# Lower weight parts in 256-column pieces only in the head stages, conditioning columns moved into the chunk stage, scan and exponentials queued behind the head

## The chip, the cores and the metric

One core of a Trainium2 chip runs the whole program. The metric is the device time of one execution in microseconds (us); the time before is the median of three runs. Engines are named as in the profile: PE (matmuls), PEld (weight loads), DVE (vector), ACT (scalar), POOL (GpSimd), SP (issues most DMAs).

## What is computed

A trunk of two layers on x (1 x 512 x 1024), all in float32. In each layer a vector c gives three conditioning vectors of 1024 (shift, scale, gate); two token mixers (HGRN2, 4 heads of 128; RWKV-7, 8 heads of 64) work on parts of one projection, and sigmoid gates merge them:

```python
for l in range(DEPTH):
    cond = jax.nn.silu(c) @ w_ada[l] + b_ada[l]
    shift, scale, gate_raw = jnp.split(cond, 3, axis=-1)
    h = x * (1.0 + scale[:, None]) + shift[:, None]
    proj = h @ w_in[l]
    p_hg, p_rw, p_gate = jnp.split(proj, [HG_COLS, HG_COLS + RW_COLS], axis=-1)
    ...
    o_hg = hgrn2_chunked(q, k_hg, i_val, log_f)
    y_rw = rwkv7_scan(r, decay, k, v, kk, a)
    ...
    merged = jax.nn.sigmoid(g_hg) * y_hg + jax.nn.sigmoid(g_rw) * y_rw
    out = merged @ w_out[l]
    x = layer_norm(DN_ALPHA * x + (1.0 + gate_raw[:, None]) * out, ln_g[l], ln_b[l])
```

## The kernel before

Activations lie transposed, 128 features on the partitions and 512 tokens in the free dimension. Every large product is split in two parts: a weight tile `raw` (128x512, four 128x128 blocks) is loaded by SP, ACT rounds it into a higher part `wh` (L122 or L244), POOL subtracts to get the lower part `wl` (L248, recorded at the helper line L127), and PE adds three matmuls per block: `wh` by the higher and lower part of the activation (L267, L268), and `wl` by the higher part (L272). Eight matmuls with `wh` come first, then four with `wl`. There are three buffers each of `raw`, `wh` and `wl`. POOL makes the lower part in pieces of 256 columns:

```python
for i in range(0, n, 256):
    x = slice(i, i + 256)
    tt(G, lo[:, x], raw[:, x], hi[:, x].bitcast(F32), ALU.subtract)
```

A layer has these stages, each a chain of small dependent work ("main") with projection matmuls woven in as filling by hand-written counts (`weave`):

- **Heads**, p = 0 to 3: `hg_head` (HGRN2 head p) and then `rw_prep` (what RWKV-7 needs for two of its heads). A head ends with a masked copy of scores (COPY_PREDICATED, L781), a copy of the last block (L806), transposes and their copy out of PSUM (L813), the state product on PE (L818), its copy (L820), two recurrent steps on DVE (L136, tile `u`) and the output product (L828, L831). In `rw_prep` DVE makes a running sum of the decays (L430, TENSOR_TENSOR_SCAN), ACT two exponentials of it (L433 into `ep`, L434 in place; both recorded at L124), and DVE the products that PE multiplies at L497. There is one buffer `ep` for all pairs of heads.
- **Inverse** of small triangular blocks (`rw_invert`) and **chunks**, c = 0 to 7 (`rw_chunk`): the recurrence of RWKV-7 over chunks of 64 tokens. In a chunk DVE scales `W` (L618), PE multiplies it (L623), the result is copied into `X`, one half by DVE and the other by ACT (L625), PE multiplies `X` (L631, L643), and DVE adds into the state `mbd` (L636, L638). The chunks are given a higher priority by 1000.
- **Branches**: for j = 0 to 7 the two branch products, the gated sum on DVE (L147, L1149), and the first half of the output product; POOL has four lower parts per j. Then the layer boundary with its norm, or the end.

The conditioning vectors are made column by column on DVE: a group is one (vector, block of 128 rows), two loads of 128x512 of `w_ada` (256 KB each, L327) and two halves, each a multiply-and-sum over 512 columns with silu(c) (`ada_col`, L308, CUSTOM_DVE in the profile), and an addition. `ada_next` computes the groups that are loaded and loads the next ones. Where a group stands in the program is set by tables of numbers: in layer 0 thirteen groups over the heads (`WAZ`) and eleven over the branches (`WAB`), in layer 1 eight over the heads (`WAO`), none in the chunks. silu(c) lies in the buffers of `mbd` and `W`, which the chunks need.

The order on each engine is made by a list scheduler from the order of the program and its own estimates. `tc.issue_after(i)` keeps what stands under it behind instruction i; without it, an instruction whose inputs are there may be put far ahead of its place in the code.

Of the kernel before, what the change touches and what calls it, by code (L numbers as in the profile page):

```python
# [18 lines left out]

WAZ = (1, 0, 2, 2, 2, 2, 2, 2)  # L20
WAO = (1, 1, 0, 1, 1, 2, 0, 2)
WAB = (2, 1, 2, 1, 2, 1, 2, 1, 1)
NWARM = 5
# [60 lines left out]
def body(ctx, tc, d):  # L84
# [41 lines left out]
    def tt(e, o, a, b, op):  # L126
        e.tensor_tensor(o, a, b, op=op)  # L127

    def mul(e, o, a, b):
        tt(e, o, a, b, ALU.mult)  # L130

# [108 lines left out]


    def split(raw, hi, lo):

        act(hi, raw, AF.Copy)  # L244
        n = raw.shape[-1]
        for i in range(0, n, 256):
            x = slice(i, i + 256)
            tt(G, lo[:, x], raw[:, x], hi[:, x].bitcast(F32), ALU.subtract)  # L248
# [69 lines left out]

    def ada_next(*groups):

        for g, w in pend:
            ada_col(*g, w)
        pend[:] = []
        for l, n, k in groups:
            w = [st("z", [128, 512]) for _ in range(2)]
            for h in range(2):
                nc.sync.dma_start(w[h], d["w_ada"][l, n, k, :, h * 512:(h + 1) * 512])  # L327
            pend.append(((l, n, k), w))

    def gate_rows(l):  # L330
# [85 lines left out]

    def rw_prep(l, p, r, k, v):
        sg, th = rw["gt"][p][:, 0], rw["gt"][p][:, 1]
# [10 lines left out]
        cum = pu()  # L429
        V.tensor_tensor_scan(cum, mask64, sg, 0.0, ALU.mult, ALU.add)  # L430
        EP = ep
        EI = cum
        act(EP[:, :, 1:65], cum.rearrange("p (c j) -> p c j", j=64), AF.Exp, scale=-KAPPA)  # L433
        act(EI, cum, AF.Exp, scale=KAPPA)  # L434
        G.tensor_copy(gam[:, p], EP[:, :, 64])
# [134 lines left out]

    def rw_chunk(l, c):

# [43 lines left out]
        for g in range(2):  # L616
            z, o = zrs[g], halves[g]
            mul(V, j3(W[z, o]), j3(py[z, o]), bc(d2[z, c4, 2 * g:2 * g + 2].rearrange("p a b -> p (a b)"), 64))  # L618
        yield
# [4 lines left out]
        for g in range(2):  # L624
            PK[1 - g](X[zrs[g], halves[g]], psa[zrs[g], halves[g]])  # L625
        yield
        if c < 7:
            pm = ps("rw")
            for p in range(4):
                for h in range(2):  # L630
                    mm(pm[64 * h:64 * h + 64, hcol(p, h)], bkt[:, hcol(p, h)], X[:, hcol(p, h)], start=p == 0, stop=p == 3)  # L631
            for h in range(2):
                hs = slice(64 * h, 64 * h + 64)
                new = pm[hs].rearrange("p (a b) -> p a b", b=128)[:, :, hs]
                if c == 0:
                    V.tensor_copy(mbd[hs, :, hs], new)  # L636
                else:
                    tt(V, mbd[hs, :, hs], new, gm[hs], ALU.add)  # L638
                if c < 6:
                    mul(G, gm[hs], mbd[hs, :, hs], bc(gam[hs, :, c + 1], 64))  # L640
        for n, (p, h) in enumerate(heads):
            y = yrs[p // 2]
            mm(py[y, hcol(p, h)], Gt[:, h, p, y], X[:, hcol(p, h)], start=False, stop=n > 5, skip_group_check=True)  # L643
# [81 lines left out]

    def hg_head(l, hd, src, outs):

# [38 lines left out]
        for n, H in enumerate(HG_LEVELS):  # L766
# [11 lines left out]
            for c in range(2):  # L778
                mm(pS[:, c * 128:(c + 1) * 128], kp[:, c * 128:(c + 1) * 128], ql[:, c * 128:(c + 1) * 128],
                   start=c == 0, stop=c == 1)  # L780
            V.copy_predicated(late(acc), hmask[:, n].rearrange("p (c b j) -> p c b j", c=4, j=H),  # L781
                              pS[:, 0:256].rearrange("p (c b j) -> p c b j", c=4, j=H))
# [29 lines left out]
        kt = u()  # L812
        A.copy(kt[:, 0:384], pT[:, 0:384])  # L813
        yield
# [173 lines left out]
    for l in range(L):  # L988
# [53 lines left out]
        if l == 0:  # L1042
            hgp = [hg_f(l, 0, fout[1]), hg_q(fout[2])]
            wad = rw_wa0(l, fout[0])
            hgp.append(hg_i(fout[3]))
            act(gh0, fout[6], AF.Tanh, scale=0.5)
            rkv = [rw_in(l, 4, fout[4]), rw_in(l, 0, fout[5])]
        else:
            hgp = [hg_f(l, 0, fout[2]), hg_q(fout[3])]
        for p in range(NP):  # L1050
            early = []
# [4 lines left out]
            else:  # L1056
                fill = itertools.chain(krv(p, rkv), rw_wa(l, wad), fqi(1, early, 1))
            weave(hg_head(l, p, hgp, oT), fill, (WHL if l else WHZ, WHG if l else WHS, WHG, WHG)[p])
            run(fill)
            ada_next(*itertools.islice(ada, (WAZ, WAO)[l][2 * p]))  # L1060
            if p == 0:
# [4 lines left out]
            else:  # L1066
                fill = itertools.chain.from_iterable(
                    [gate(j) for j in range(5)] + [zrw(p) for p in range(NP)] + [zhg(p) for p in range(NP)] +
                    [gate(j) for j in range(5, KT)])
            weave(rw_prep(l, p, rkv[1], rkv[0], rkv[2]), fill, WPR)  # L1070
            ada_next(*itertools.islice(ada, (WAZ, WAO)[l][2 * p + 1]))
            if p < 3:
                run(fill)
            rkv = []
        ada_next()
        G.memset(mbd, 0.0)
        inv = rw_invert()
# [293 lines left out]
```

## Time and profile before

| | |
|---|---|
| median of 3 runs | 1013.33 us (1008.05 to 1017.07) |
| the profiled execution | 1013.57 us, span 1011.8 us |
| PE busy | 939.3 us (93%) |
| DVE busy | 711.7 us (70%) |
| POOL busy | 632.4 us (63%) |
| ACT busy | 452.2 us (45%) |
| DMA, mean | 112 GB/s |
| granted PE clock, mean | 0.991 |

The span is the time from the first instruction to the last; 1.8 us lie around it. Busy shares are means over stages that differ: the idle time of PE, 72.5 us in all, is what a change of order can win, and the views by stage say where it lies. A clock of 1.00 is the level of 2.4 GHz, and 0.5 that of 1.2 GHz.

### The profile page before, as it was taken

What the parts mean: (1) busy time and instruction counts of PE and PEld (TensorE: products, weight loads), DVE (VectorE), ACT (ScalarE), POOL (GpSimd) and SP (SyncE); (2) the same over time, 40 slices, a digit from 0 to 9 for tenths busy, and PEclk for the clock granted to TensorE, in tenths of its full rate; (3) what the DMA queues carried; (4) which work ended last, traced back from release to release, by engine and by line L of the source; (5) the groups of instructions that cost most, each with busy time, mean ns of one, the idle gap of its engine ahead of it and who ended that gap; (6) DMA issues with size and microseconds to landing.
All of it is one profiled execution on the core that took longest, in us unless ns stands there. A gap on an engine that the chain in (4) does not pass through costs nothing.

```text
span 1011.8 us, 17028 instructions
## 1 busy us (share of the span) xinstructions
PE 939.3 (93%) x6132; PEld 751.6 (74%) x6132; DVE 711.7 (70%) x1265; ACT 452.2 (45%) x920; POOL 632.4 (63%) x738
## 2 busy tenths in 40 slices
PE   7877889999999999999989979999999999999997
PEld 3656768887877777776877868778788777787776
DVE  7889997769974443588777895867699344436667
ACT  3356445556334335333445645446632443453421
POOL 5366646556655557768646566666754566686865
PEclk9999999999999999999999999999999999999999
DMA  8824532222321112665632632232233111254322
GB/s 315 306 63 136 177 126 74 88 80 80 97 75 45 52 46 65 186 213 169 186 132 63 205 87 77 70 94 63 64 99 90 53 43 53 85 177 157 115 74 83
DMA packets 61750, 112.85 MB, mean 112 GB/s; under 512 B 6865, under 2 KB 11361, under 8 KB 61666
## 3 DMA queue, kind: packets, MB, share of 16 engines
q1 hardware_dynamic: 57778, 105.12, 34.1%
q10 hardware_dynamic: 3888, 6.64, 2.0%
q8 instruction: 48, 0.79, 0.3%
q14 instruction: 36, 0.29, 0.1%
HBM read 106.49 MB, written 5.25 MB: 110 GB/s over the span
## 4 chain that ended last, share of the span: by engine, by line
PE 47%; DVE 24%; POOL 9%; DMA 7%; issue 7%; ACT 6%; POOLq 0%; SPq 0%; DVEq 0%; ACTq 0%
PE ppj L272 11%; PE ppj L267 10%; PE ppj L268 10%; POOL wl L127 5%; DVE u L127 4%; DVE z L308 2%; DVE B L308 2%; DVE hl L127 2%; DMA raw<-in_w_out 2%; DMA z<-in_w_ada 2%; ACT wh L122 2%; PE prw L589 2%; POOL hl L127 1%; PE prw L608 1%; DVE pu L136 1%
## 5 line engine op out<-in xcount | busy, mean ns | idle before, releaser
L127 POOL TENSOR_TENSOR wl<-raw,wh 128x256 fp32r<-128x256 f32 x460 | 384.5, 859 | 245.1 <-ACT wh L122 158.5
L122 ACT ACTIVATE wh<-raw 128x512 fp32r<-128x512 f32 (+1 forms) x233 | 144.0, 622 | 162.6 <-PE ppj L268 87.2
L267 PE MATMUL ppj<-B,wh 128*128 128x512 f32 x432 | 175.4, 406 | 5.3 <-DVE u L136 2.2
L268 PE MATMUL ppj<-B,wh 128*128 128x512 f32 x432 | 172.3, 399 | 0.0
L267 PE MATMUL ppj<-A,wh 128*128 128x512 f32 x400 | 161.1, 403 | 0.2 <-ACT wh L122 0.2
L268 PE MATMUL ppj<-A,wh 128*128 128x512 f32 x400 | 159.6, 399 | 0.0
L272 PE MATMUL ppj<-B,wl 128*128 128x512 f32 x432 | 125.9, 401 | 0.6 <-DVE dvsh L127 0.4
L272 PE MATMUL ppj<-A,wl 128*128 128x512 f32 x400 | 116.9, 401 | 4.6 <-POOL wl L127 4.6
L267 PEld LDWEIGHTS ppj<-B,wh 128*128 128x128 f32 x432 | 81.9, 190 | 24.0 <-ACT wh L122 3.8
L272 PEld LDWEIGHTS ppj<-B,wl 128*128 128x128 f32 x432 | 80.3, 190 | 19.0 <-POOL wl L127 2.4
L268 PEld LDWEIGHTS ppj<-B,wh 128*128 128x128 f32 x432 | 82.0, 190 | 14.9
L272 PEld LDWEIGHTS ppj<-A,wl 128*128 128x128 f32 x400 | 73.3, 188 | 22.8 <-POOL wl L127 8.1
L267 PEld LDWEIGHTS ppj<-A,wh 128*128 128x128 f32 x400 | 75.5, 189 | 16.0 <-ACT wh L122 0.6
L268 PEld LDWEIGHTS ppj<-A,wh 128*128 128x128 f32 x400 | 75.7, 189 | 13.7
L127 POOL TENSOR_TENSOR hl<-hl,u 128x256 f32<-128x256 f32 x40 | 31.9, 797 | 20.7 <-DVE u L774 7.8
L127 DVE TENSOR_TENSOR W<-prw,d 64x256 f32<-64x256 f32 x32 | 13.5, 422 | 36.9 <-PE prw L613 26.0
L136 DVE SCALAR_TENSOR_TENSOR pr<-ppj,prm,pr 128x511 f32<-128x511 f32 x22 | 16.4, 747 | 31.8 <-ACT pr L124 31.8
L127 DVE TENSOR_TENSOR t<-t,t 128x144 f32<-128x144 f32 (+29 forms) x62 | 35.1, 566 | 2.1
L308 DVE CUSTOM_DVE_ANT_0 z<-z,mbd,prm 128x512 f32<-128x512 f32 x32 | 31.8, 995 | 3.9 <-DMA z<-in_w_ada 3.8
L127 DVE TENSOR_TENSOR hl<-hl,u 128x256 f32<-128x256 f32 x64 | 32.6, 524 | 1.4 <-ACT u L792 1.3
L308 DVE CUSTOM_DVE_ANT_0 z<-z,W 128x512 f32<-128x512 f32 x32 | 29.0, 905 | 2.7 <-DMA z<-in_w_ada 2.7
L127 DVE TENSOR_TENSOR G<-prw,cc 128x512 f32<-128x512 f32 x32 | 20.6, 684 | 12.0 <-PE prw L589 11.8
(480 smaller groups left out, 1967.4 us busy)
## 6 DMA issues: line engine op xcount, KB each, us to landing
raw<-in_w_in SPq DMA_DIRECT2D x182, 256.0 KB, 2.6
z<-in_w_ada SPq DMA_DIRECT2D x64, 256.0 KB, 3.2
B<-in_w_ada SPq DMA_DIRECT2D x16, 512.0 KB, 5.9
raw<-in_w_br SPq DMA_DIRECT2D x32, 256.0 KB, 2.7
raw<-in_w_out SPq DMA_DIRECT2D x32, 256.0 KB, 2.6
u<-in_x SPq DMA_DIRECT2D x8, 256.0 KB, 4.5
o<-in_w_in SPq DMA_DIRECT2D x14, 128.0 KB, 4.2
t<-in_xt SPq DMA_DIRECT2D x6, 256.0 KB, 3.2
```

The lines of the kernel that those rows point to most:

```text
L122: A.activation(out, in_, f, scale=scale)
L127: e.tensor_tensor(o, a, b, op=op)
L136: V.scalar_tensor_tensor(o, a, s, b, op0=op0, op1=op1)
L267: yield mm(o, w, xh, start=half == 0 and k == 0, stop=False)
L268: yield mm(o, w, xl, start=False, stop=False)
L272: yield mm(o, w, xh, start=False, stop=half == n - 1 and k == 3)
L308: V.tensor_tensor_reduce(out=w[h], in0=w[h], in1=silc[h], scale=0.5, scalar=0.0 if h else init, op0=ALU.mult, op1=ALU.add, accum_out=part[ ...
L589: mm(pg[h][:, p * 128:(p + 1) * 128], BK[p][hs, ch], ZR[p][hs, ch], start=p == 0, stop=p == 3)
L608: mm(py[:, p * 128:(p + 1) * 128], ZR[p][:, ch], mbd[:, p], start=p == 0, stop=False)
```

## The change

Four things change. (1) `split` makes the lower part in one piece of 512 columns, except between the start and the end of the head stages, where pieces stay at 256: 316 pieces become 158. (2) The conditioning groups move: in layer 0 one after each half of a head stage (8), one in each chunk (8), one in each j of the branches (8); in layer 1 all 8 in the chunks. In a chunk the first half stands behind the scaling of `W`, the second behind the addition into `mbd`; the loads go into tiles of the tag `u` (6 buffers) instead of `z` (4). Since the chunks overwrite the buffers that hold silu(c), ACT copies it into a tile `hl` and a tile `pr` ahead of them. (3) The scan is held behind the head's last COPY_PREDICATED, the exponentials behind the copy at L813. (4) In a chunk ACT takes the first half of the copy into `X`, and DVE the second.

```diff
-WAZ = (1, 0, 2, 2, 2, 2, 2, 2)
-WAO = (1, 1, 0, 1, 1, 2, 0, 2)
-WAB = (2, 1, 2, 1, 2, 1, 2, 1, 1)
+WAZ = (1, 1, 1, 1, 1, 1, 1, 1)
+WAB = (1, 1, 1, 1, 1, 1, 1, 1, 0)
...
+    piece = [512]
+
     def split(raw, hi, lo):
 
         act(hi, raw, AF.Copy)
-        n = raw.shape[-1]
-        for i in range(0, n, 256):
-            x = slice(i, i + 256)
+        for i in range(0, raw.shape[-1], piece[0]):
+            x = slice(i, min(i + piece[0], raw.shape[-1]))
...
-    def ada_next(*groups):
+    def ada_next(*groups, tag="z"):
...
-            w = [st("z", [128, 512]) for _ in range(2)]
+            w = [st(tag, [128, 512]) for _ in range(2)]
...
+    def ada_parts():
+        (g, w), = pend
+        pend[:] = []
+        return ada_col(*g, w, False)
...
-    def rw_prep(l, p, r, k, v):
+    def rw_prep(l, p, r, k, v, after):
...
-        V.tensor_tensor_scan(cum, mask64, sg, 0.0, ALU.mult, ALU.add)
+        with tc.issue_after(after[0].ins):
+            V.tensor_tensor_scan(cum, mask64, sg, 0.0, ALU.mult, ALU.add)
...
-        act(EP[:, :, 1:65], cum.rearrange("p (c j) -> p c j", j=64), AF.Exp, scale=-KAPPA)
-        act(EI, cum, AF.Exp, scale=KAPPA)
+        with tc.issue_after(after[1].ins):
+            act(EP[:, :, 1:65], cum.rearrange("p (c j) -> p c j", j=64), AF.Exp, scale=-KAPPA)
+            act(EI, cum, AF.Exp, scale=KAPPA)
...
-    def rw_chunk(l, c):
+    def rw_chunk(l, c, side):
...
-            mul(V, j3(W[z, o]), j3(py[z, o]), bc(d2[z, c4, 2 * g:2 * g + 2].rearrange("p a b -> p (a b)"), 64))
+            last = mul(V, j3(W[z, o]), j3(py[z, o]), bc(d2[z, c4, 2 * g:2 * g + 2].rearrange("p a b -> p (a b)"), 64))
+
+        with tc.issue_after(last.ins):
+            side(0)
...
-            PK[1 - g](X[zrs[g], halves[g]], psa[zrs[g], halves[g]])
+            last = PK[g](X[zrs[g], halves[g]], psa[zrs[g], halves[g]])
...
-                    tt(V, mbd[hs, :, hs], new, gm[hs], ALU.add)
+                    last = tt(V, mbd[hs, :, hs], new, gm[hs], ALU.add)
...
+        with tc.issue_after(last.ins):
+            side(1)
...
-            V.copy_predicated(late(acc), hmask[:, n].rearrange("p (c b j) -> p c b j", c=4, j=H),
+            last = V.copy_predicated(late(acc), hmask[:, n].rearrange("p (c b j) -> p c b j", c=4, j=H),
...
-        A.copy(kt[:, 0:384], pT[:, 0:384])
+        ends[:] = last, A.copy(kt[:, 0:384], pT[:, 0:384])
...
+        piece[:] = [256]
         for p in range(NP):
...
         ada_next()
+
+        piece[:] = [512]
+        keep = [hl(), st("pr", [128, 512])]
+        for h in range(2):
+            A.copy(keep[h], silc[h])
+        silc[:] = keep
         G.memset(mbd, 0.0)
...
         for c in range(8):
-            weave(rw_chunk(l, c), fill, WCH, 1000)
+            ada_next(*itertools.islice(ada, 1), tag="u")
+            weave(rw_chunk(l, c, ada_parts()), fill, WCH, 1000)
```

ACT at the end of head 1 of layer 0, before. `pu_1800` is the running sum of head pair 2, `hl` the scores of head 1, `wh` higher weight parts:

```order
L122 ACTIVATE wh_1332<-raw_1330 128x512
L124 ACTIVATE pr_1222<-ppj_1143,dvomm_93 128x512
L122 ACTIVATE wh_1369<-raw_1367 128x512
L124 ACTIVATE ep<-pu_1800 128x8x64
L806 COPY hl_1065<-prw_1255 64x2x64 x2
L813 COPY u_1264<-phg_1260 128x384
L124 ACTIVATE pu_1800<-pu_1800 128x512
L820 COPY u_1283<-prw_1279 128x128
```

The same place after the change (L819, L826 and L833 are the former L806, L813 and L820; `pu_1325` is the running sum of pair 1 itself):

```order
L121 ACTIVATE wh_1373<-raw_1371 128x512
L819 COPY hl_1069<-prw_1259 64x2x64 x2
L826 COPY u_1268<-phg_1264 128x384
L123 ACTIVATE ep<-pu_1325 128x8x64
L123 ACTIVATE pu_1325<-pu_1325 128x512
L833 COPY u_1287<-prw_1283 128x128
```

Before, the exponential of the next pair stood ahead of the two copies; now that of this pair stands behind them and ahead of the copy of the state product.

DVE in head 2 of layer 1, before. `A` are products of `rw_prep`, `u_6710` the recurrent steps of the head:

```order
L781 COPY_PREDICATED hl_6465<-hmask,prw_6623 128x16x16
L136 SCALAR_TENSOR_TENSOR A_5433<-pr_6611,prm,ep 128x4x64
L127 TENSOR_TENSOR pu_6796<-pr_6611,pu_6796 128x512
L136 SCALAR_TENSOR_TENSOR A_5433<-pr_6611,prm,ep 128x4x64
L127 TENSOR_TENSOR A_5434<-pu_6796,pu_6767 128x4x128
L781 COPY_PREDICATED hl_6465<-hmask,phg_6645 128x8x32
L136 SCALAR_TENSOR_TENSOR pr_6688<-ppj_6614,prm,pr_6688 128x511
L127 TENSOR_TENSOR A_5433<-pr_6688,ep 128x4x128
L136 SCALAR_TENSOR_TENSOR u_6710<-u_6710,u_6467,prw_6706 128x128 x2
```

The same place after the change:

```order
L794 COPY_PREDICATED hl_6368<-hmask,prw_6526 128x16x16
L794 COPY_PREDICATED hl_6368<-hmask,phg_6548 128x8x32
L437 SCALAR_TENSOR_TENSOR pu_6662<-mask_86,t_1050_5490 128x512
L126 TENSOR_TENSOR pu_6691<-pr_6514,pu_6691 128x512
L135 SCALAR_TENSOR_TENSOR pr_6591<-ppj_6517,prm,pr_6591 128x511
L135 SCALAR_TENSOR_TENSOR A_5356<-pr_6514,prm,ep 128x4x64
L126 TENSOR_TENSOR A_5356<-pr_6591,ep 128x4x128
L135 SCALAR_TENSOR_TENSOR u_6613<-u_6613,u_6370,prw_6609 128x128
```

The four instructions that stood between the last two masked copies now stand behind the last one, the scan (L437) joins them, and two products with `ep` come ahead of the head's first recurrent step.

DVE in chunk 4 of layer 0, before. `W`, `X` and `mbd` are those of the chunk, `u_3639` belongs to a projection of the filling:

```order
L127 TENSOR_TENSOR W_3635<-prw_3615,d_152 64x256 x2
L136 SCALAR_TENSOR_TENSOR u_3639<-u_3639,ppj_3521 128x512
L625 COPY X_902<-prw_3655 64x256
L127 TENSOR_TENSOR mbd<-prw_3671,gm 64x4x64 x2
L127 TENSOR_TENSOR G_3707<-prw_3697,cc 128x512
```

The same place after the change (the L308 rows are the two halves of a group and the reading of their sums):

```order
L126 TENSOR_TENSOR W_3607<-prw_3587,d_152 64x256 x2
L308 ISA u_3547,sm_3551<-u_3547,hl_2392,prm 128x512
L308 ISA sm_3551 128x1
L135 SCALAR_TENSOR_TENSOR u_3612<-u_3612,ppj_3488 128x512
L636 COPY X_902<-prw_3627 64x256
L126 TENSOR_TENSOR mbd<-prw_3643,gm 64x4x64 x2
L308 ISA u_3548,sm_3551<-u_3548,pr_2393 128x512
L308 ISA sm_3551 128x1
L126 TENSOR_TENSOR dvsh_116<-sm_3551 128x1
L126 TENSOR_TENSOR G_3686<-prw_3676,cc 128x512
```

One half of a group now stands between the scaling of `W` and DVE's copy into `X`, the other ahead of the next chunk's products.

## Rows read from the trace of the kernel before

**Rows 1.** The page, busy time, share of the span and instructions by engine.

```profile
PE 939.3 (93%) x6132; PEld 751.6 (74%) x6132; DVE 711.7 (70%) x1265; ACT 452.2 (45%) x920; POOL 632.4 (63%) x738
```

**Rows 2.** Windows: stretch, length, busy PE, PEld, DVE, ACT, POOL (instructions), clock, DMA share, GB/s.

```profile
110.00:155.00 45.00, 38.23 (x219) 31.32 (x219) 42.66 (x92) 21.61 (x53) 26.75 (x29) 0.96 0.45 144
305.00:395.00 90.00, 88.87 (x896) 68.16 (x894) 38.04 (x72) 36.23 (x70) 52.82 (x64) 1.00 0.17 48
415.00:490.00 75.00, 69.13 (x287) 53.85 (x286) 56.89 (x92) 25.36 (x43) 55.12 (x61) 0.98 0.60 190
912.00:990.00 78.00, 72.85 (x311) 57.02 (x310) 51.89 (x62) 25.32 (x42) 57.18 (x62) 1.00 0.36 110
```

**Rows 3.** Timeline, layer 0, head 1: start, duration, engine, line; idle before and its releaser.

```profile
131.50 1.30 DVE L308 CUSTOM_DVE_ANT_0 z<-z,mbd,prm 128x512 f32<-128x512 f32 x1
...
133.40 0.42 DVE L781 COPY_PREDICATED hl<-hmask,phg 128x256 f32<-128x256 uint8 x1
...
134.44 0.63 ACT L124 ACTIVATE ep<-pu 128x512 f32<-128x512 f32 x1 [3.19 <-DVE B L127]
...
135.52 0.48 ACT L813 COPY u<-phg 128x384 f32<-128x384 f32 x1
...
136.05 1.11 PE L818 MATMUL prw<-hl,u 128*128 128x128 f32 x6 [3.98 <-ACT u L813]
```

**Rows 4.** Windows right behind two waits of PE, columns as above.

```profile
130.00:140.00 10.00, 6.02 (x28) 4.82 (x27) 10.00 (x25) 4.19 (x10) 4.97 (x5) 0.83 0.36 123
600.00:605.00 5.00, 4.72 (x20) 4.07 (x20) 4.33 (x12) 1.57 (x4) 2.40 (x4) 0.66 0.30 86
```

**Rows 5.** Timeline, layer 0, first `rw_prep`, PE.

```profile
105.72 0.69 PE L497 MATMUL prw<-B,B 64*64 64x64 f32 x32 [0.88 <-DVE B L136]
```

**Rows 6.** Windows of line L308 alone: stretch, length, DVE busy (instructions), clock, DMA, GB/s.

```profile
107.00:155.00 48.00, 15.53 (x36) 0.96 0.46 145
...
555.00:600.00 45.00, 12.65 (x32) 0.98 0.52 154
```

**Rows 7.** Timeline, layer 1, end of the first `rw_prep` and start of head 1, PE.

```profile
585.58 0.50 PE L465 MATMUL prw<-u,bonesr 128*128 128x512 f32 x1 [2.21 <-DVE u L127]
...
599.56 0.46 PE L750 MATMUL phg<-u,u 128*128 128x128 f32 x2 [2.55 <-DVE u L127]
```

**Rows 8.** Timeline, layer 1, head 2.

```profile
663.95 0.43 DVE L781 COPY_PREDICATED hl<-hmask,phg 128x256 f32<-128x256 uint8 x1
...
665.56 0.94 PE L818 MATMUL prw<-hl,u 128*128 128x128 f32 x6 [0.72 <-ACT u L813]
```

**Rows 9.** Timeline of a chunk of layer 0.

```profile
342.62 0.88 DVE L127 TENSOR_TENSOR W<-prw,d 64x256 f32<-64x256 f32 x2 [3.46 <-issue]
...
343.62 0.69 DVE L136 SCALAR_TENSOR_TENSOR u<-u,ppj 128x512 f32<-128x512 f32 x1
...
344.53 0.42 DVE L625 COPY X<-prw 64x256 f32<-64x256 f32 x1 [0.23 <-PE prw L623]
...
345.79 0.69 PE L631 MATMUL prw<-X,bkt 128*64 128x64 f32 x16
```

**Rows 10.** Waits of PE for the copy into `X`: us in total, times, longest.

```profile
PE prw L631 <- ACT X L625: 2.7, 5, 0.6
```

**Rows 11.** Line L308: ns min/median/max, first and last start.

```profile
L308 DVE CUSTOM_DVE_ANT_0 z<-z,mbd,prm x32: 728/956/1311, 83.4 to 593.7; 128x512 f32<-128x512 f32 x32
```

**Rows 12.** The page, DMA issues: KB each, median us from issue to landing.

```profile
z<-in_w_ada SPq DMA_DIRECT2D x64, 256.0 KB, 3.2
```

**Rows 13.** Lines on POOL: branches of layer 1, then whole span; busy us, mean ns.

```profile
L127 POOL TENSOR_TENSOR wl<-raw,wh 128x256 fp32r<-128x256 f32 x42 | 38.5, 944 | 8.5 <-ACT wh L122 8.5
...
L127 POOL TENSOR_TENSOR B<-u,B 128x512 fp32r<-128x512 f32 x8 | 10.7, 1345 | 9.3 <-ACT B L122 5.4 <-DVE sm L136 3.8
```

**Rows 14.** Timeline, branches of layer 0, then of layer 1, PE.

```profile
431.34 0.47 PE L267 MATMUL ppj<-B,wh 128*128 128x512 f32 x1 [0.95 <-DVE dvsh L127]
...
953.23 0.73 PE L272 MATMUL ppj<-A,wl 128*128 128x512 f32 x2 [1.45 <-POOL wl L127]
```

More of the change, by code (lines that the diff above doesn't have):

```diff
@@ L126, in tt @@
     def tt(e, o, a, b, op):
-        e.tensor_tensor(o, a, b, op=op)
+        return e.tensor_tensor(o, a, b, op=op)
     def mul(e, o, a, b):
-        tt(e, o, a, b, ALU.mult)
+        return tt(e, o, a, b, ALU.mult)
     def ts(e, o, a, s1, s2, op0, op1):
@@ L635, in rw_chunk @@
                 if c == 0:
-                    V.tensor_copy(mbd[hs, :, hs], new)
+                    last = V.tensor_copy(mbd[hs, :, hs], new)
                 else:
-                    tt(V, mbd[hs, :, hs], new, gm[hs], ALU.add)
+                    last = tt(V, mbd[hs, :, hs], new, gm[hs], ALU.add)
                 if c < 6:
                     mul(G, gm[hs], mbd[hs, :, hs], bc(gam[hs, :, c + 1], 64))
+        with tc.issue_after(last.ins):
+            side(1)
         for n, (p, h) in enumerate(heads):
@@ L724, in hg_i, with hg_head @@
         return iv
-    def hg_head(l, hd, src, outs):
+    def hg_head(l, hd, src, outs, ends):
         (f, K), Qb = src[:2]
@@ L1057, in body @@
                 fill = itertools.chain(krv(p, rkv), rw_wa(l, wad), fqi(1, early, 1))
-            weave(hg_head(l, p, hgp, oT), fill, (WHL if l else WHZ, WHG if l else WHS, WHG, WHG)[p])
+            weave(hg_head(l, p, hgp, oT, ends := []), fill, (WHL if l else WHZ, WHG if l else WHS, WHG, WHG)[p])
             run(fill)
-            ada_next(*itertools.islice(ada, (WAZ, WAO)[l][2 * p]))
+            if l == 0:
+                ada_next(*itertools.islice(ada, WAZ[2 * p]))
             if p == 0:
@@ L1069, in body @@
                     [gate(j) for j in range(5, KT)])
-            weave(rw_prep(l, p, rkv[1], rkv[0], rkv[2]), fill, WPR)
-            ada_next(*itertools.islice(ada, (WAZ, WAO)[l][2 * p + 1]))
+            weave(rw_prep(l, p, rkv[1], rkv[0], rkv[2], ends), fill, WPR)
+            if l == 0:
+                ada_next(*itertools.islice(ada, WAZ[2 * p + 1]))
             if p < 3:
```

## The prediction

> **What bounds the kernel now.** I read the page first, then windows by stage, and then the timeline wherever PE stood for over half a microsecond. The page says that PE is busy for 939.3 us [rows 1], and the span is 1011.8 us, so 72.5 us of idle time are all that a new order can win; no matmul is added or removed. The windows say where such time lies [rows 2]. In the chunks of layer 0 PE is busy for 88.87 of 90 us: nothing is to be won there, but DVE has 52 us to spare. In the end of the heads DVE is nearly full (42.66 of 45 us) and PE loses 6.8 us. In the branches PE loses 5.87 us of 75 (layer 0) and 5.15 of 78 (layer 1). So the change takes work off DVE where DVE is short of time, and puts it where DVE is idle; the question is whether the new place lies on a path too.
>
> My sum is made against the profiled execution, 1013.57 us (span 1011.8 and 1.8 around it), which is 0.24 above the median of three, 1013.33. Those three spread over 0.9%, so about 1% is what a measurement can tell from no change.
>
> **(a) The end of head 1, layer 0.** PE waits 3.98 us at the state product for the copy at L813 [rows 3]. ACT reaches that copy late because the next pair's exponential stands ahead of it, and this exponential had itself left ACT idle for 3.19 us, waiting on products that DVE makes (there is one `ep`, and its last readers are those of the pair before). The order now has both copies ahead of the exponential. What is late next is the last masked copy, which ends at 133.82; ahead of it DVE did a half of a group (1.30 us at 131.50), which leaves this place. From the masked copy to PE there remain the copy at L806 and that at L813 (0.48), some 1.0 us. Gain 3.0. Behind the wait the granted clock falls: 0.83 over 10 us [rows 4], which is 10 x 0.17 / 0.5 = 3.4 us at the level of 1.2 GHz, and work done in it takes twice as long, so up to 1.7 us. A wait of 1 us elsewhere is not followed by such a stretch; I take half, 0.8. Together **-3.8** (bounds -1.0, if the masked copy is no earlier, and -5.7).
>
> **(b) First `rw_prep`, layer 0.** PE stands 0.88 us for a product of DVE [rows 5]. The scan of the next pair is no longer ahead of it. **-0.9** (0 to -0.9). The groups themselves don't help here: the order has the first eight at their old places, and only the five behind them leave. That is why I count none of the 15.53 us of L308 [rows 6] as such.
>
> **(c) Heads 0 and 1, layer 1.** Here all groups leave: 12.65 us of DVE between 555 and 600 us [rows 6]. PE waits 2.21 us at the end of the first `rw_prep` and 2.55 at the start of head 1, each time for a DVE product [rows 7]. With a quarter of DVE's time gone there, I keep 0.7 us of the 4.76: **-4.0**. The clock behind the second wait is 0.66 over 5 us [rows 4], 5 x 0.34 / 0.5 = 3.4 us at the lower level; half of 1.7 again, **-0.9** (both: -2.0 to -6.5).
>
> **(d) Later heads.** The wait of 0.72 us at the state product [rows 8] goes as in (a). Against it, the scan and two products with `ep` now stand between the last masked copy and the first recurrent step. The output products L828 and L831 queue behind that step; while it waits, PE has projections as filling, but they run out towards the end of a head. In the trace of before this order does not occur. Bounds: -2 (six heads with a third of a microsecond each) to +2 (a scan or a product in the way in half of them, at the 0.69 us of a 512-wide operation [rows 9]). I take **-0.5**, nearer to the gain since the filling covers most such steps now.
>
> **(e) Chunks.** *Copy into X.* PE's wait for ACT's half of it, 2.7 us in all [rows 10], goes, since that half is now first and DVE's second: -2.7. *The first half of a group* now stands between W and DVE's half of X. From the timeline of a chunk [rows 9]: W ends at 343.50, the addition for the projection takes 0.69, the copy 0.42, and PE starts L631 at 345.79. A half takes 0.73 to 1.31 us [rows 11], so the new copy ends at 343.50 + (0.73 to 1.31) + 0.69 + 0.42 = 345.34 to 345.92: 0.45 us to spare, or 0.13 late. Sixteen chunks make 0 to 2.1 us; I take 1.2, since other chunks have their addition later. *The second half* stands ahead of the next chunk's products with `cc`; PE has filling there, and the cover is thick (98.7% busy). If it were gone, it would cost 0.96 us a chunk. DVE's load rises from 38 to some 54 of 90 us. ACT's two copies of silu(c) ahead of the chunks lie beside work of DVE and POOL in the norm; ACT is busy for 45%, and I cost them at nothing (1 us if `wh` is late there). Sum of chunks **-1.5** (-2.7 to +2.1).
>
> **(f) Pieces of 512 columns.** A piece of 256 takes 944 ns on POOL in the branches, and eight 512-wide subtractions elsewhere 1345 ns [rows 13]. So a lower part takes 1.35 instead of 1.89 us, 0.54 less; four per j and eight j make 17 us of POOL per layer. POOL is busy for 55 to 57 us of 75 to 78 there [rows 2], and PE waits for `wl` for 1.45 us in layer 1 [rows 14]. I let half of the 5.15 us idle go, -2.5. In layer 0 the same for a part (-1.0), and the wait for a sum of the conditioning, 0.95 us [rows 14], since fewer groups stand there, eight instead of eleven: -1.0. Against it: PE can start with a piece of 256 after 0.94 us, and with the whole only after 1.35. That costs 0.4 us where POOL is just in time; eight matmuls with `wh` come first, and they cover it unless POOL is behind, when 0.54 per part is won. **-4.5** (0 to -8).
>
> **The sum** is -3.8 - 0.9 - 4.9 - 0.5 - 1.5 - 4.5 = -16.1. A PE that comes earlier meets its next release earlier than that is there; where I saw several small waits in a row, a part of each gain comes back at the next. I keep three quarters: -12.1, and 1013.6 - 12.1 = **1001.5 us**. The bounds of the terms alone, added, give -31 to +1; they will not all fall on one side, and three quarters of a sum of -10 and of -26 make 1006 and 994.
>
> **Rival 1: half is absorbed, 1008 us.** What delays the heads is a chain of DVE products, not the queue; then (a) and (c) yield their lower bounds (-3.0 instead of -8.7), (f) half (-2.3), and the rest stays: -3.0 - 0.9 - 0.5 - 1.5 - 2.3 = -8.2, and three quarters of that are -6. For it: DVE is 95% busy at the end of the heads in layer 0, and the scan and exponentials, behind the head now, make `rw_prep` start later. Against it: the releaser of the largest wait is ACT, in a queue that the change reorders.
>
> **Rival 2: halves and pieces hold each other up, 1008 to 1015 us.** POOL's subtractions and DVE's halves both read two operands from SBUF. A half takes 728 ns at best and 1311 at worst [rows 11], so something beside it stretches it by up to 0.58 us, while W and X keep their times. If a half waits for the rest of a piece, a piece of 1.35 us in the place of 0.94 lengthens that. At worst, the whole piece: 343.50 + 1.35 + 0.73 + 0.69 + 0.42 = 346.69, 0.90 us behind PE's start, and 14.4 us over sixteen chunks. With the other gains (three quarters of -14.6 and of -2.7, together -13.0) the time is 1013.6 - 13.0 + 14.4 = 1015; POOL is busy for 59% of the chunks, so half of it, 1008, is likelier than all. The largest stretch seen, 0.58, is under a piece of 256, which speaks against waiting for whole pieces.
>
> The Trainium skill ("SBUF — State Buffer", section "SBUF: two separate sides") states this as a rule: DVE and GpSimd share a port pair, a DVE operation with two SBUF inputs needs it against a GpSimd operation that reads SBUF, and the one that starts second is fully blocked until the first ends. By that rule the time would be that of this rival; the trace agrees in so far as the halves are stretched, and doesn't show one stretched by a whole piece.
>
> **Rival 3, slower: a half waits for its load, 1027 us.** DVE takes its queue in order. A half in a chunk needs 256 KB that take 3.2 us from issue to landing [rows 12], in a tile of the ring `u`, which the projections use as well; the load is issued in the chunk that uses it, by SP, behind loads of weights that wait for their own buffers. If it is late, the copy into X stands behind the half, and L631, the state and the next chunk behind that. Lateness up to 0.45 us costs nothing; 2 us in every chunk cost 16 x (2.0 - 0.45) = 25 us, and 1013.6 - 11.5 + 25 = 1027. It ends on the slower side from 0.45 + 11.5/16 = 1.2 us per chunk. Against it: the chunks move only 48 GB/s [rows 2], SP has time, and the load may be put ahead by most of a chunk of 11 us.
>
> That the change doesn't do what it says, I exclude: the order shows the groups, copies and exponentials at their new places.
>
> **How the numbers follow.** Forecast, 994 to 1006 around 1001.5: 0.64, of which 0.52 lies under 1003.2 (faster by over 1%) and 0.12 above. Rival 1: 0.18, within 1%. Rival 2: 0.11, within 1%. Rival 3: 0.07, slower. So faster 0.52, same 0.41, slower 0.07. The range runs from 994 to 1011, past rival 1 and the milder half of rival 2; the rest of that, rival 3 and the tail below make up the two in ten outside.
>
> **What the profile after would show.** (a) and (d): the exponential into `ep` behind the copy of L813 (new L826), and PE waiting there for 1 us or less; if the wait is still over 2, the masked copy is the cause. (c): no L308 in the heads of layer 1, and PE's waits at L465 and L750 under 0.6 us together. (e): waits of PE for X from DVE instead of ACT, under 2 us in all; if they are over 5, rival 2 (halves of 1.3 us and more) or 3 (DVE idle ahead of the half, released by a DMA). (f): `wl` pieces of some 1.35 us and no wait of over 1 us for them in the branches; if pieces take 1.8 us, (f) is nothing. I am wrong if PE's idle time is above 68 us.

## The result, and the profile after

The changed kernel takes 996.25 us in the median of four runs (994.91 to 997.83), against 1011.93 for the kernel before on the same chip: ratio 0.9835, 95% interval 0.9811 to 0.9858. The profiled execution took 997.83 us, with a span of 996.0. The page, busy time by engine after:

```profile
PE 943.5 (95%) x6132; PEld 762.2 (77%) x6132; DVE 733.2 (74%) x1265; ACT 453.8 (46%) x924; POOL 602.9 (61%) x580
```

PE's idle time is 996.0 - 943.5 = 52.5 us, 20 less than before [rows 1]. Yet the span is only 15.8 us shorter: PE is busy for 4.2 us longer with the same 6132 matmuls, beside a mean granted clock of 0.977 instead of 0.991. Ahead of head 1 alone its busy time grew by 5.3 us, at a clock of 0.95 and 0.93 where it was 1.00; the stretches there are as long as before, so this cost no time. To see where the time went I cut both traces at the same instructions and compared the stretches. The cuts are the first matmul of a head, DVE's first transposition of the inverse, the first matmul with X in the chunks, the first matmul of the output product in the branches, and PE's first transposition of the boundary:

| stretch | before | after | change |
|---|---|---|---|
| layer 0, head 0 with its `rw_prep` | 48.4 | 48.1 | -0.3 |
| layer 0, head 1 | 44.1 | 38.7 | -5.4 |
| layer 0, heads 2 and 3 | 78.3 | 77.6 | -0.7 |
| layer 0, inverse and first chunk up to its X | 72.6 | 79.5 | **+6.9** |
| layer 0, rest of the chunks | 116.6 | 112.8 | -3.8 |
| layer 0, branches | 73.2 | 69.1 | -4.1 |
| boundary | 42.6 | 43.8 | +1.2 |
| layer 1, head 0 | 56.3 | 51.0 | -5.3 |
| layer 1, heads 1 to 3 | 128.4 | 121.9 | -6.5 |
| layer 1, inverse and first chunk up to its X | 72.4 | 79.2 | **+6.8** |
| layer 1, rest of the chunks | 119.2 | 117.7 | -1.5 |
| layer 1, branches and end | 92.2 | 89.1 | -3.1 |

Gains of 30.7 us, and 14.9 given back, nearly all in the two inverses, which no term of the prediction looked at. Windows of the kernel after, columns as in [rows 2]. The rows are head 1, the inverse in three parts (DVE's transpositions, products and sums; the small matmuls; the first chunk up to its X), the chunks from the first product of X to the last, and the branches of layer 0, then head 0, head 2 and the branches of layer 1:

```profile
115.60:154.30 38.70, 38.38 (x223) 32.43 (x224) 30.88 (x63) 21.64 (x51) 22.96 (x28) 0.96 0.27 78
231.90:278.40 46.50, 46.50 (x214) 38.53 (x214) 44.33 (x66) 19.87 (x37) 22.41 (x18) 1.00 0.33 95
278.40:297.60 19.20, 18.12 (x307) 14.04 (x305) 15.05 (x10) 6.22 (x10) 7.46 (x7) 0.91 0.20 64
297.60:311.40 13.80, 11.19 (x76) 8.13 (x75) 5.00 (x10) 5.16 (x9) 6.02 (x5) 0.75 0.21 64
311.40:378.20 66.80, 66.80 (x699) 51.45 (x698) 46.34 (x87) 24.41 (x49) 42.05 (x39) 1.00 0.35 105
424.20:493.30 69.10, 67.52 (x297) 55.19 (x296) 55.68 (x87) 25.06 (x42) 45.49 (x32) 1.00 0.60 184
537.10:588.10 51.00, 47.21 (x263) 37.64 (x263) 38.77 (x66) 32.05 (x71) 33.23 (x40) 1.00 0.24 70
630.90:673.80 42.90, 42.25 (x246) 35.39 (x246) 30.38 (x60) 23.29 (x56) 29.46 (x34) 1.00 0.27 80
906.90:996.00 89.10, 78.66 (x361) 63.73 (x359) 65.15 (x94) 27.02 (x46) 54.07 (x37) 0.97 0.31 101
```

And three stretches of the kernel before that the prediction had not opened (products of the inverse, first chunk, head 2 of layer 1):

```profile
238.30:280.20 41.90, 41.90 (x195) 34.72 (x194) 39.70 (x66) 18.03 (x34) 24.91 (x31) 1.00 0.32 95
301.10:310.90 9.80, 8.36 (x74) 6.05 (x73) 4.35 (x8) 4.80 (x8) 4.89 (x7) 1.00 0.22 59
644.60:689.80 45.20, 43.07 (x247) 35.19 (x246) 31.79 (x59) 23.16 (x55) 28.53 (x34) 1.00 0.28 76
```

In the first part of the inverse, the products' stretch, DVE makes 31 products and 31 sums in turn, each of which needs the one before. DVE is nearly full there in both kernels (39.70 of 41.90, 44.33 of 46.50), so the stretch has DVE's length. PE is full there too, but with filling, the projection matmuls that are woven in: 214 matmuls instead of 195. What it takes early is missing behind. PE then waits for 1.08 us behind the first two of the inverse's matmuls and for 2.61 in the first chunk, and the granted clock is 0.91 and 0.75 where it was 1.00. Timeline of the kernel after, PE:

```profile
283.11 1.19 PE L555 MATMUL prw<-ar 32*32 32x32 f32 x62 [1.08 <-DVE ar L544]
302.26 1.11 PE L609 MATMUL prw<-cc,W 128*128 128x128 f32 x4 [2.61 <-ACT ar L574]
```

Why DVE needs longer is seen when its rows are read beside POOL's. Timeline of the kernel after, inverse of layer 0, DVE and POOL:

```profile
249.25 0.95 DVE L126 TENSOR_TENSOR t<-t,t 128x192 f32<-128x192 f32 x1
250.24 0.36 DVE L541 TENSOR_REDUCE t<-t 128x16 f32<-128x192 f32 x1
250.64 0.38 DVE L126 TENSOR_TENSOR t<-t,t 128x208 f32<-128x208 f32 x1
...
251.40 1.29 POOL L126 TENSOR_TENSOR wl<-raw,wh 128x512 fp32r<-128x512 f32 x1 [1.40 <-PE ppj L272]
251.45 1.48 DVE L126 TENSOR_TENSOR t<-t,t 128x224 f32<-128x224 f32 x1
252.96 0.39 DVE L541 TENSOR_REDUCE t<-t 128x16 f32<-128x224 f32 x1
253.39 0.41 DVE L126 TENSOR_TENSOR t<-t,t 128x240 f32<-128x240 f32 x1
```

Products of 208 and 240 columns take 0.38 and 0.41 us; the one of 224, which starts 0.05 us behind a piece of 512 columns on POOL, takes 1.48 and ends 0.24 us behind that piece. The same instruction before the change, between two pieces, took 0.39, and one of 192 columns that met a piece of 256 took 0.85:

```profile
255.09 1.55 POOL L127 TENSOR_TENSOR wl<-raw,wh 128x256 fp32r<-128x256 f32 x2 [1.23 <-ACT wh L122]
255.18 0.85 DVE L127 TENSOR_TENSOR t<-t,t 128x192 f32<-128x192 f32 x1
...
257.31 0.39 DVE L127 TENSOR_TENSOR t<-t,t 128x224 f32<-128x224 f32 x1
```

Over both inverses the 62 products take 35.1 us before and 44.3 after (mean 566 and 715 ns). The sums between them (L541, one input) took 26.4 us in both kernels.

### The profile page after: what moved, and what is told of

Its sections match the earlier page's. It is cut to its first block, busy times and chain, and to the rows that moved or that the text cites. A ratio compares the mean times of both kernels' runs of the same rounds, so it can differ in the third digit from the quotient of the medians.

```text
span 996.0 us, 16762 instructions
## 1 busy us (share of the span) xinstructions
PE 943.5 (95%) x6132; PEld 762.2 (77%) x6132; DVE 733.2 (74%) x1265; ACT 453.8 (46%) x924; POOL 602.9 (61%) x580
## 4 chain that ended last, share of the span: by engine, by line
PE 63%; DVE 25%; DMA 4%; ACT 3%; issue 3%; POOL 2%; SPq 0%; DVEq 0%; POOLq 0%; ACTq 0%
PE ppj L272 14%; PE ppj L267 13%; PE ppj L268 13%; DVE t L126 5%; DVE t L541 3%; DVE B L308 2%; DVE t L533 2%; PE prw L597 2%; DVE u L126 1%; POOL wl L126 1%; PE prw L616 1%; PE ppj L1194 1%; PE ppj L1196 1%; PE ppj L1195 1%; PE prw L621 1%
## 5 line engine op out<-in xcount | busy, mean ns | idle before, releaser
L126 POOL TENSOR_TENSOR wl<-raw,wh 128x256 fp32r<-128x256 f32 (+1 forms) x321 | 348.1, 1099 | 268.0 <-ACT wh L121 135.3
L267 PE MATMUL ppj<-A,wh 128*128 128x512 f32 x400 | 163.1, 408 | 0.0
L268 PE MATMUL ppj<-A,wh 128*128 128x512 f32 x400 | 161.4, 403 | 0.0
L268 PEld LDWEIGHTS ppj<-B,wh 128*128 128x128 f32 x432 | 82.1, 190 | 14.9
L272 PEld LDWEIGHTS ppj<-A,wl 128*128 128x128 f32 x400 | 75.3, 193 | 20.2 <-POOL wl L126 4.5
L267 PEld LDWEIGHTS ppj<-A,wh 128*128 128x128 f32 x400 | 76.7, 192 | 16.0 <-ACT wh L121 0.3
L268 PEld LDWEIGHTS ppj<-A,wh 128*128 128x128 f32 x400 | 76.9, 192 | 14.1
L126 DVE TENSOR_TENSOR t<-t,t 128x144 f32<-128x144 f32 (+29 forms) x62 | 44.3, 715 | 2.1
L516 ACT COPY X<-prw 64x128 f32<-64x128 f32 x64 | 16.7, 261 | 25.4 <-PE prw L512 24.7
L541 DVE TENSOR_REDUCE t<-t 128x4 f32<-128x4 f32 (+30 forms) x62 | 26.4, 425 | 2.1
L126 DVE TENSOR_TENSOR u<-u 128x256 f32<-128x256 f32 (+6 forms) x56 | 25.5, 456 | 0.7
```

What stands on the lines that cost most here:

```text
L126: return e.tensor_tensor(o, a, b, op=op)
L267: yield mm(o, w, xh, start=half == 0 and k == 0, stop=False)
L268: yield mm(o, w, xl, start=False, stop=False)
L272: yield mm(o, w, xh, start=False, stop=half == n - 1 and k == 3)
L516: A.copy(rw["vtm"][2 * t + e][r:r + 64, p * 128:(p + 1) * 128], pT[64 * e:64 * e + 64, t * 128:(t + 1) * 128])
L541: V.tensor_reduce(blk(R, t, [32, j]), pv, axis=AX.X, op=ALU.add)
```

## The experiments

Two theories were put to the chip first. **Theory 1:** the wide pieces hold up DVE in the inverse. **Theory 2:** what is new around the first chunk (the copies of silu(c), the first group) makes the loss.

**Pieces of 256 through the inverse.**

```diff
-        piece[:] = [512]
         keep = [hl(), st("pr", [128, 512])]
...
         weave(inv, fill, WT)
+        piece[:] = [512]
         for c in range(8):
```

> Pieces of 256 columns are kept until the inverse is done; chunks and branches have 512, all else as after the change. Theory 1 (in the inverse, DVE's products over two SBUF operands wait for a whole piece on POOL; the longer inverse runs PE out of filling and its clock falls): the products and sums go back from 37.5 to about 33 us in layer 0, the waits of PE around the first chunk from 3.7 to about 1.4 us per layer, the granted clock there to 1.00; some 6 us per layer are won and the time is about 984 us (981 to 988). Theory 2 (the copies of silu(c) and the first group, new around the first chunk, make the loss there): the first chunk stays at 13.8 us and the time at 996 (994 to 998).

Measured: 982.84 us, ratio to before 0.9694 (0.9669 to 0.9719). Windows of this kernel, products of the inverse and first chunk:

```profile
230.38:272.31 41.93, 41.93 (x194) 34.74 (x194) 39.72 (x67) 18.00 (x34) 25.40 (x32) 1.00 0.35 96
293.10:302.70 9.60, 8.43 (x74) 6.08 (x73) 5.00 (x10) 5.16 (x9) 4.53 (x4) 1.00 0.22 55
```

The products' stretch of layer 0 is back at 41.9 us, the first chunk at 9.6 with the clock at 1.00, though the copies and the group are still there. Theory 1 stands, theory 2 is out.

**Pieces of 128 there**, as the last but with `piece[:] = [128]` ahead of `keep`.

> As the kernel with 256 columns through the inverse, but 128 columns there. Theory 1: a product waits at most for a piece of 128; the products and sums of the inverse fall below the 32.9 us of before, towards 29 (their own times: 13.2 us of products and 13.2 of sums, with the gaps between). PE was full in that stretch already, so the time is only that of the 256 kernel, within 2 us, unless the 1.4 us of waiting at the first chunk goes too. Theory 2: 996.

Measured: 978.5 us, 0.9661 (0.9636 to 0.9686). The same windows:

```profile
229.36:269.18 39.82, 39.82 (x186) 33.00 (x185) 37.61 (x67) 17.38 (x33) 30.28 (x61) 1.00 0.35 98
292.10:300.30 8.20, 8.20 (x74) 6.16 (x73) 4.29 (x9) 4.01 (x7) 3.94 (x3) 1.00 0.10 33
```

The stretch loses another 2.1 us, and in the first chunk of layer 0 PE no longer waits at all. The median is lower than with 256, but the two intervals still overlap by a little.

**The kernel before with pieces of 512 in the inverse alone**, the reverse of the first (`split` reads `piece` here, which starts at 256).

```diff
         ada_next()
+        piece[:] = [512]
         G.memset(mbd, 0.0)
...
         weave(inv, fill, WT)
+        piece[:] = [256]
```

> The kernel before, with pieces of 512 columns from the end of the heads to the end of the inverse and nothing else changed. Theory 1: the products and sums of the inverse go from 32.9 to 37.5 us, PE runs out of filling and the clock falls around the first chunk: some 6 to 7 us per layer, 1025 us (1020 to 1028). If the loss of the changed kernel needs its other parts (copies of silu(c), groups in the chunks): 1013.

Measured: 1026.56 us, 1.013 (1.0111 to 1.0148); its 62 products take 44.3 us, as after the change. The loss needs nothing else of the change.

**Pieces of 256 everywhere.**

```diff
-    piece = [512]
+    piece = [256]
...
-        piece[:] = [512]
         keep = [hl(), st("pr", [128, 512])]
```

> Pieces of 256 columns everywhere, the other three parts of the change kept. Theory 1: the inverse is as with 256 there (some 12 us won against the changed kernel), and the branches lose what the wide pieces gave, 6 us in layer 0 and 3 in layer 1: about 993 us (989 to 997). Theory 2: only the loss in the branches, 1005.

Measured: 989.31 us, 0.9767 (0.974 to 0.9795). Faster than the change itself: as it was made, part one lost more in the inverse than it won behind. Against the kernel that has 512 from the chunks on (982.84), the branches are longer by 1.9 us in layer 0 (73.3 and 71.4) and 2.5 in layer 1 (91.9 and 89.4).

**Scan and exponentials free**, and **the scan alone free.**

```diff
-        with tc.issue_after(after[0].ins):
+        if True:
             V.tensor_tensor_scan(cum, mask64, sg, 0.0, ALU.mult, ALU.add)
...
-        with tc.issue_after(after[1].ins):
+        if True:
             act(EP[:, :, 1:65], ...
```

(The second kernel has only the first of these two edits.)

> Scan and exponentials are not held behind the head; all else as after the change. If the hold made the gain in the heads (the wait of 3.98 us at the state product, and the 0.5 to 0.7 us at the state products and scores of later heads): about 9 us are lost, 1005 us. If the groups that left the heads made it: within 2 us of 996.

> The exponentials are held behind the copy of the transposes, the scan is free; all else as after the change. If ACT's queue (the exponential that waits ahead of the head's last copies) is the cost of the kernel without holds: 996 to 998. If the scan on DVE is (it goes ahead of the head's masked copies, with the products that follow it): 1004 to 1008.

Measured: 1007.84 us, 0.9944 (0.9925 to 0.9963) with both free; 997.1, 0.9856 (0.9835 to 0.9878) with the scan free. So the hold of the exponentials is worth some 9 to 11 us and that of the scan nothing measurable. (The exponentials need the scan, so a held scan holds them too; they were not tried free behind a held scan.) How it works is seen at head 1 of layer 0, both free:

```profile
127.28 0.74 DVE L135 SCALAR_TENSOR_TENSOR B<-pr,prm,ep 128x512 f32<-128x512 f32 x1
...
132.99 0.42 DVE L794 COPY_PREDICATED hl<-hmask,phg 128x256 f32<-128x256 uint8 x1
...
134.03 0.63 ACT L123 ACTIVATE ep<-pu 128x512 f32<-128x512 f32 x1 [2.58 <-DVE B L126]
...
135.11 0.48 ACT L826 COPY u<-phg 128x384 f32<-128x384 f32 x1
...
135.64 0.94 PE L831 MATMUL prw<-hl,u 128*128 128x128 f32 x6 [2.46 <-ACT u L826]
```

and in the changed kernel:

```profile
130.15 0.44 DVE L794 COPY_PREDICATED hl<-hmask,phg 128x256 f32<-128x256 uint8 x1
...
132.29 0.48 ACT L826 COPY u<-phg 128x384 f32<-128x384 f32 x1
132.66 0.64 ACT L123 ACTIVATE ep<-pu 128x512 f32<-128x512 f32 x1
...
133.24 0.83 PE L831 MATMUL prw<-hl,u 128*128 128x128 f32 x6
```

The exponential no longer stands ahead of the copy, and the last masked copy too comes 2.8 us earlier. In the free kernel products with `ep` are done ahead of it (127.28); in the changed one they can't be, since `ep` isn't made yet.

**The copy into X as before.**

```diff
-            last = PK[g](X[zrs[g], halves[g]], psa[zrs[g], halves[g]])
+            last = PK[1 - g](X[zrs[g], halves[g]], psa[zrs[g], halves[g]])
```

> The copy into X as before (DVE the first half, ACT the second), all else as after the change. If the new assignment is what won PE's 2.7 us of waits for X (2.7 us of gain, as in the prediction's term e): 999 us, with waits at L631 again. If the half of a group ahead of DVE's copy decides, DVE's copy is now the first to be wanted and late in every chunk by up to 0.7 us: 1003 to 1007. If neither matters: 996.

Measured: 1020.1 us, 1.0065 (1.0052 to 1.0078), worse than all three cases. PE's waits for X are 8.2 us at L642 (5.0 for ACT's half, 3.2 for DVE's) and 1.8 at L656; that explains a part. The edit also changed the scheduler's order on PE: in some chunks L642 no longer stands in one row of 16 but in turns with L597. Timeline of this kernel, PE:

```profile
349.07 0.33 PE L642 MATMUL prw<-X,bkt 128*64 128x64 f32 x2
349.33 0.48 PE L597 MATMUL prw<-B,B 64*128 64x128 f32 x2
349.75 0.33 PE L642 MATMUL prw<-X,bkt 128*64 128x64 f32 x2
350.00 0.48 PE L597 MATMUL prw<-B,B 64*128 64x128 f32 x2
```

Such a chunk takes 13.7 us (from 347.7 to 361.4) against 11.1 in the changed kernel; the first chunks, where L642 stands in two rows of 8 and waits, 12.5. How the 24 us divide between waiting and turns isn't settled. So this run says that the kernel as the scheduler makes it loses with the old assignment, and not what the assignment is worth by itself.

**The groups as before.**

```diff
-            if l == 0:
-                ada_next(*itertools.islice(ada, WAZ[2 * p]))
+            ada_next(*itertools.islice(ada, (WAZ, WAO)[l][2 * p]))
...
-            ada_next(*itertools.islice(ada, 1), tag="u")
-            weave(rw_chunk(l, c, ada_parts()), fill, WCH, 1000)
+            weave(rw_chunk(l, c, lambda h: None), fill, WCH, 1000)
```

(with the three old tables, and without the copies of silu(c))

> The conditioning groups as before (13 over the heads and 11 over the branches of layer 0, 8 over the heads of layer 1, none in the chunks, no copies of silu(c)), the other three parts kept. If groups in the heads cost what the prediction's terms b and c say: the waits of PE in head 0 and at head 1 of layer 1 come back (5 us or more there), some 1 to 3 us at head 1 of layer 0, 1 in the branches of layer 0; the chunks win at most 1 us back: about 1004 us (1001 to 1007). If the hold alone made the heads short: 996 to 998.

Measured: 1005.21 us, 0.9926 (0.9905 to 0.9947). Head 0 of layer 1 takes 56.1 us again (51.0 after the change), with waits of 2.65 and 2.10 us; head 1 of layer 0 42.5 (38.7). From the first product of X to the last in layer 0, the chunks without groups take 66.5 us, with them 66.8: the groups' halves cost 0.3 us there, and about as much in layer 1.

At head 1 of layer 0 the last masked copy is as late as before the change (133.25 and 133.40 us, against 130.15), though both holds are in place, and PE waits behind it. Timeline of this kernel:

```profile
133.25 0.42 DVE L795 COPY_PREDICATED hl<-hmask,phg 128x256 f32<-128x256 uint8 x1
...
134.85 0.94 PE L832 MATMUL prw<-hl,u 128*128 128x128 f32 x6 [1.82 <-ACT u L827]
```

**Towards a better version.** Three kernels with 128 columns in the inverse: 128 in the heads too; 256 in the chunks; both. The edits are cut against the kernel with 128 in the inverse alone:

```diff
-        piece[:] = [256]
+        piece[:] = [128]
         for p in range(NP):
...
-        piece[:] = [512]
+        piece[:] = [256]
         for c in range(8):
...
+        piece[:] = [512]
         o_hg, y_rw = big(tag_r), big(tag_r)
```

> As the kernel with 128 columns through the inverse, but 128 in the heads too. If DVE's operations over two SBUF operands wait for pieces in the heads as they do in the inverse, and lie on PE's path there: 1 to 4 us less than 978.5. If DVE has time to spare in the heads now, or POOL with four pieces (4 x 0.52 us against 2 x 0.89) falls behind: 978 to 983.

> The changed kernel with 128 columns through the inverse, 256 in the heads and the chunks, 512 from the end of the chunks. If DVE's halves and sums in the chunks wait for wide pieces on PE's path: the 1.8 and 0.7 us by which the kernel with 256 everywhere was shorter from the second chunk to the branches are won, 976 us. If PE's filling covers the chunks: 978.5.

> As the last one, with 128 columns in the heads too: 1.7 us less than it, as between the two kernels that differ by that alone (978.5 and 976.8): 974.5 if both gains are there and add up, 976.8 if only the heads' is.

Measured: 976.79 us, 0.9637 (0.9622 to 0.9651); 978.72, 0.966 (0.9643 to 0.9677); 976.11, 0.9629 (0.9608 to 0.965). The chunks' width makes no difference that can be measured. The heads' may be worth 2 us; the intervals overlap. The last kernel takes 0.9629 / 0.9835 = 0.979 of the changed one's time.

## Why the prediction was right, and where it wasn't

The time was forecast at 1001.5 us and came out at 996.25, inside the range, on the side forecast, and PE's idle time is 52.5 us, below the 68 that would have said that I am wrong. That the sum came so close is in part luck. The stretches gained 30.7 us, where the terms had 16.1 and the sum kept 12.1; the two inverses, which had no term, took 13.7 back. One addition was wrong: the lower bounds of the terms make -25.8 and not -31. The range was worked from -26, so nothing else hangs on it.

**Right.** (c): -4.9 forecast, head 0 of layer 1 gave -5.3, and 5.1 of it went when the groups were put back.

**(a)**: -3.8 forecast, -5.4 measured, inside its bounds. The wait of 3.98 us [rows 3] is gone, and the granted clock from 130 to 140 us is 1.00 where it was 0.83 [rows 4]. Its lower bound of -1.0 was for a masked copy that comes no earlier. The kernel with the old groups and both holds shows that case: the copy is there at 133.25 us, and head 1 takes 42.5 us, 1.6 less than before. With the new groups and no holds it takes 41.3, and with both 38.7. So moving the groups off DVE is worth at least as much there as the holds, though the working named ACT's queue first. The run without holds shows a second path for the holds too, by DVE's products with `ep` ahead of the masked copy.

**(e)** was mis-sized: -1.5 forecast for both layers, with bounds of -2.7 and +2.1. From the first product of X to the last the chunks are shorter by 1.3 us in layer 0 (68.1 to 66.8) and by 2.0 in layer 1 (68.8 to 66.8), 3.3 together. The waits for X [rows 10] are gone as forecast; the halves of the groups, put at 1.2 us, cost 0.6 by the kernel with the groups as before. The other 2.0 us of the table's rows for the rest of the chunks lie behind the last product, in no term.

**(b)**, -0.9 forecast: -0.3. The wait at that product [rows 5] is 1.61 us instead of 0.88, though PE comes to it at 103.89 instead of 104.84. With the scan free L505 starts at 102.3 instead of 105.5, and head 1 at 114.4 instead of 115.6: here the scan's hold costs about what it was meant to give. Head 1 then takes 39.5 us instead of 38.7, which gives most of it back.

**(d)** was mis-sized: -0.5 forecast, with bounds of -2 and +2; measured -0.7 in layer 0 and -6.5 in layer 1, together past the bound. I priced the wait of 0.72 us [rows 8] as the whole gain and set the scan and products against it. A head of layer 1 lost 2.1 us to idle time before (45.20 - 43.07), in many pieces of which that wait is one, and 0.65 after (42.90 - 42.25). The holds made this gain: head 2 of layer 1 takes 45.1 us with both free, and 42.9 with the groups put back. The two products that I feared in the recurrent steps' way lay, in the kernel without holds, ahead of the masked copy instead, which is worse.

**(f)** came out larger than forecast, within its bounds (0 to -8): -4.5 forecast, -4.1 and -3.1 measured, 7.2 together, of which the kernel with 256 everywhere gives 1.9 and 2.5 us to the pieces. In layer 1 waits for `wl` remain, the longest 0.95 us, where 1.45 was seen before [rows 14]. In layer 0 one wait remains, and it is longer than any of before; the wide pieces make it. DVE's subtraction for the lower part of the merged activations starts behind a piece and takes 1.75 us, against 0.68 where it meets none. Timeline of the kernel after:

```profile
424.62 1.75 DVE L126 TENSOR_TENSOR A<-u,A 128x512 fp32r<-128x512 f32 x1
...
426.42 0.50 PE L1131 MATMUL prw<-wh,A 128*128 128x512 f32 x1 [1.58 <-DVE A L126]
```

The pieces take 1.47 and 1.52 us in the mean in the branches of the two layers and not 1.35, where they take 1.29 in the inverse unless they meet a DVE product. DVE's operations hold them up in turn: a longer piece starts while a DVE operation with two SBUF inputs runs, and ends some 1.15 us behind it. Timeline of the kernel after, branches of layer 0, where the two engines take turns for 4 us:

```profile
435.83 0.74 DVE L308 CUSTOM_DVE_ANT_0 z<-z,mbd,prm 128x512 f32<-128x512 f32 x1
435.95 1.78 POOL L126 TENSOR_TENSOR wl<-raw,wh 128x512 fp32r<-128x512 f32 x1 [0.97 <-ACT wh L121]
...
436.51 1.77 DVE L308 CUSTOM_DVE_ANT_0 z<-z,W 128x512 f32<-128x512 f32 x1
437.93 1.49 POOL L126 TENSOR_TENSOR wl<-raw,wh 128x512 fp32r<-128x512 f32 x1 [0.20 <-ACT wh L121]
...
438.21 1.76 DVE L126 TENSOR_TENSOR A<-u,A 128x512 fp32r<-128x512 f32 x1
```

**Absorption.** I kept three quarters of each gain. Apart from (b), the stretches gave the whole term or more, so nothing of the kind is seen in them.

**What failed** is the working of "(f) Pieces of 512 columns": it was priced in the branches alone. The pieces also change the inverse and the chunks, and the step "what bounds the kernel now" had no window of the inverse: PE is full there, so I took it for a stretch without a price. But PE is full with filling, and DVE's chain sets its length. It cost 6.9 and 6.8 us. Of the 4.6 us by which the products' stretch of layer 0 grew, all is in the products: (44.3 - 35.1) / 2 = 4.6. The rest is what follows when filling has been used up: waits of 3.7 us where 1.4 were, and the low clock in the first chunk.

**The rivals.** Rival 2 had the right mechanism, in the wrong place. In the chunks halves do wait for wide pieces: the first halves take 1345 ns in the mean, the second ones 760. Of the 16 first halves, 14 start behind a piece of 512 or another operation of that width on POOL, and end 0.55 us behind its end. Lines of the kernel after, L308:

```profile
L308 DVE CUSTOM_DVE_ANT_0 u<-u,hl,prm 128x512 f32<-128x512 f32 x16 | 21.5, 1345 | 0.3
...
L308 DVE CUSTOM_DVE_ANT_0 u<-u,pr 128x512 f32<-128x512 f32 x16 | 12.2, 760 | 0.5
```

It costs 0.3 us a layer at most, as the kernel with the groups as before shows: ACT's half of X lets PE begin, and DVE's comes while it runs. Timeline of the kernel after, chunk 3 of layer 0:

```profile
341.93 1.29 POOL L126 TENSOR_TENSOR wl<-raw,wh 128x512 fp32r<-128x512 f32 x1 [4.07 <-issue]
342.39 1.37 DVE L308 CUSTOM_DVE_ANT_0 u<-u,hl,prm 128x512 f32<-128x512 f32 x1
...
343.38 0.37 ACT L636 COPY X<-prw 64x256 f32<-64x256 f32 x1 [0.95 <-PE prw L634]
...
344.52 0.43 DVE L636 COPY X<-prw 64x256 f32<-64x256 f32 x1
...
344.64 0.82 PE L642 MATMUL prw<-X,bkt 128*64 128x64 f32 x16
```

I argued against it by the largest stretch seen, 0.58 us, which is less than a piece of 256. That was weak: nothing in it told when each half had met a piece, and how much of one. The inverse, where DVE is a chain of 31 products per layer, had the answer in the trace before: 0.85 us for 192 columns beside a piece, 0.39 for 224 without one.

The rule of the Trainium skill that I cited ("SBUF — State Buffer", section "SBUF: two separate sides") says that the one that starts second is blocked to the end of the first. The traces agree: 1.48 us for 0.39 beside a piece of 1.29. They agree as well on an operation with one SBUF input: the sums keep their time, also the 14 that start while POOL works. I gave the rule 0.11 and one place; its price belongs to each stage in which DVE's two-operand work is a chain.

Rival 1 (half absorbed) is out, by the stretches of the heads. Rival 3 (a half waits for its load) as well: DVE is idle for 0.3 and 0.5 us in all ahead of the 32 halves in chunks.

## What to carry to other kernels

A stage in which the matmul engine is full is not free of price: if it is full with filling, the chain that it waits for sets how much filling is left behind. Where GpSimd (POOL) and VectorE (DVE) both read two operands from SBUF, try small pieces on GpSimd next to a VectorE chain, and large ones where TensorE waits for GpSimd itself. Here that was 128 or 256 in the inverse, worth some 13 to 18 us, and 512 in the branches, worth some 4. Cost a changed instruction size in every stage that issues it, and not only in the one for which it is meant.

## What the runs showed of the hardware that wasn't expected

A VectorE product of 224 columns took 1.48 us beside a GpSimd piece of 1.29 us that had started 0.05 earlier, and 0.39 alone. The multiply-and-sum over 512 columns behaves likewise (1.37 us behind a piece, 0.74 ahead of one). It goes both ways: a GpSimd piece of 512 that started while such an operation ran took 1.78 us instead of 1.29. In the kernel with the copy into X as before, matmuls with weights of 128x64 and of 64x128 in turns of two took 0.33 and 0.48 us a turn, while 16 in a row of the first take 0.82 us in the changed kernel, or 0.10 per two.
